# Two of four weight-block sums of a seven-product square built by an accumulating DMA from GpSimd instead of VectorE

## The chip, the cores and the metric

The kernel runs on 1 core of one Trainium2 chip. The metric is the device time of one execution in microseconds. The kernel before took 1205.96 us (median of 3 runs, 1202.22 to 1206.86).

## What is computed

One decoder layer on 256 tokens of width 2048: a mixer (pooling heads and RWKV-7 heads), then a squared-ReLU MLP, then a gate with per-layer embeddings, and a final norm. All weights and activations are float32. The change lies in the MLP:

```python
h2 = rms_norm(x, mlp_norm[i])
x = x + jnp.square(jax.nn.relu(h2 @ w_ffn_up[i])) @ w_ffn_down[i]
```

with `w_ffn_up` 2048 x 8192 and `w_ffn_down` 8192 x 2048.

## The kernel before, in words

**Precision.** TensorE multiplies fp32r operands. To keep float32 accuracy each operand is split into a high part (ScalarE copies it to fp32r, `wh`) and a low part (VectorE subtracts the copy from the source, `wl`). A product is three matmuls: high x high, high x low, low x high (L1100 to L1102). So every weight that is loaded costs one or two ScalarE copies (128x512 each) and one VectorE subtraction (128x1024) before TensorE can use it.

**Stages.** The mixer comes first. Then the MLP runs in two halves of the 8192 hidden columns (`ffn_half`, L1172). Each half computes FFN-up for eight groups of hidden columns (`gemm_wide`), squares them, and then makes two sweeps of FFN-down (`down_sweep`, L1078), one for each 1024 of the 2048 output columns: sweeps 1 and 2 for the first half, 3 and 4 for the second. The last sweep also keeps weights for the gate (`keep`, L1039) and transposes the residual for the next stage (L1007, `between`).

**A sweep** goes over 16 squares (`kp`, L1122). A square is 256 tokens by 256 hidden rows by 1024 output columns, seen as 2 x 2 blocks. The weights of a square are two raw tiles, rx and ry, of 128 x 1024 float32 (512 KB each); rx holds W11 and W12, ry holds W21 and W22, each 128 x 512. They are loaded on SyncE's queue into a pool of three buffers (`load_raw`, L140). Ten squares (twelve in the last sweep) take the ordinary eight block products, 24 matmuls. The squares in `SEVEN` = 1, 3, 6, 8, 11, 13 (1, 3, 6, 11 in the last sweep; 22 in all) use a Strassen-Winograd form with seven products, 21 matmuls. For it the activations are summed while FFN-up runs (`activation_sums`, L1063), and the weights in the sweep by VectorE, in the tile `t_` (one buffer of 128 x 2048, slot a1):

```python
t1 = W12 - W11          # L1140
t3 = W22 - W12          # L1141
t2 = t3 + W11           # L1142
t4 = W21 - t2           # L1143
```

Then t1 and t3 are split together (`halves_of` "c", L1111 and L1112), and t2 and t4 (`halves_of` "d", into own tiles). The split tiles `wh` and `wl` of the pool have three buffers each.

**Order of the work.** Every engine works through a queue of its own in order. The Tile framework makes that order when the kernel is built, by program order and priorities (`tc.high_priority`), and adds the semaphore waits that the data and the buffers need. SyncE's queue holds the loads; a load waits for the buffer it writes. GpSimd's queue is used only at the start, for constants.

**After the last seven-product square of a sweep** (L1155 to L1167) the products that only the seven-product form fills are added to the residual `xr` with the scale `s2` (`add`, L1120); s2 is the inverse mean square of the norm, computed once in the first half of FFN-up (`inv_ms`, L1028). The other four banks are added at the end of the sweep.

Of the kernel before, what the change touches and what calls it, by code (L numbers as in the profile page):

```python
# [9 lines left out]
F32 = mybir.dt.float32  # L10
F32R = mybir.dt.float32r
AF = mybir.ActivationFunctionType
ALU = mybir.AluOpType
# [27 lines left out]
def trunk(  # L41
# [19 lines left out]
    nc = tc.nc  # L61

    const = ctx.enter_context(tc.tile_pool(name="const", bufs=1))
# [6 lines left out]
    def mm_bank(name):  # L70
        return psm.tile([128, 512], F32, tag="mm", name=name)
# [68 lines left out]
    def load_raw(src, n, name):  # L140
        raw = wp.tile([128, 1024], F32, tag="raw", name=f"raw_{name}")
        nc.sync.dma_start(raw[:, 0:n], src)
        return raw
# [11 lines left out]
    def split_sb(h_ap, l_ap, src_ap):  # L155
        nc.scalar.activation(h_ap, src_ap, AF.Copy)  # L156
        nc.vector.tensor_tensor(l_ap, src_ap, h_ap.bitcast(F32), op=ALU.subtract)  # L157
# [93 lines left out]
    def a8(slot, name, dt=F32):  # L251
        return act.tile([128, 2048], dt, tag=f"a{slot}", name=name)
# [713 lines left out]
    fp = ctx.enter_context(tc.tile_pool(name="fp", bufs=1))  # L966
# [57 lines left out]


    s2 = const.tile([128, 2], F32, name="s2sq")

    def inv_ms():  # L1028
        ss2 = rms_stat(xr, "n2")
        nc.vector.tensor_scalar(s2, ss2, 1.0 / D, NORM_EPS, op0=ALU.mult, op1=ALU.add)  # L1030
        nc.vector.reciprocal(s2, s2)

    h3_box = []

# [22 lines left out]

    SEVEN = (1, 3, 6, 8, 11, 13)  # L1060
    s_slots = (0, 2, 5)

    def activation_sums(box, kp, r):  # L1063

        i = SEVEN.index(kp)
        if i % 2 == 0:
            box[kp] = box[SEVEN[min(i + 1, len(SEVEN) - 1)]] = a8(s_slots[i // 2], f"S{kp}", F32R)
        st = box[kp][:, i % 2 * 1024 : i % 2 * 1024 + 1024]
        t_ = fp.tile([128, 1024], F32, tag="junk", bufs=1, name=f"s{kp}")
        s1, s2_, s3, s4 = (t_[:, j * 128 : (j + 1) * 128] for j in range(4))  # L1070
        a11, a21, a12, a22 = (r[:, j * 128 : (j + 1) * 128] for j in range(4))
        nc.vector.tensor_tensor(s1, a21, a22, op=ALU.add)
        nc.vector.tensor_tensor(s3, a11, a21, op=ALU.subtract)
        nc.vector.tensor_tensor(s2_, s1, a11, op=ALU.subtract)
        nc.vector.tensor_tensor(s4, a12, s2_, op=ALU.subtract)
        split_sb(st[:, 0:512], st[:, 512:1024], t_[:, 0:512])

    def down_sweep(hf, pair, ys, sboxes, hooks=(), between=None, seven=SEVEN):  # L1078

        nm = f"d{hf}{pair}"  # L1080
        hooks = dict(hooks)
        b2, b4, b3, bx = (mm_bank(f"{nm}_b{i}") for i in range(4))
        w16, w57 = (wide_bank(f"{nm}_w{i}") for i in range(2))
        b1, b6, b5, b7 = w16[:, 0], w16[:, 1], w57[:, 0], w57[:, 1]
        todo = {"2": 0, "3": 0, "4": 0, "x": 0, "1": 0, "5": 0, "6": 0, "7": 0}
        banks = {"2": b2, "3": b3, "4": b4, "x": bx, "1": b1, "5": b5, "6": b6, "7": b7}
        for kp in range(16):
            if kp in seven:
                for n in "1234567":
                    todo[n] += 1  # L1090
            else:
                for n in "234x":
                    todo[n] += 2
        left = dict(todo)

        def prod(n, a_, w_):
            first, last = left[n] == todo[n], left[n] == 1
            left[n] -= 1
            (ah, al), (wh, wl) = a_, w_
            nc.tensor.matmul(banks[n], ah, wh, start=first, stop=False)  # L1100
            nc.tensor.matmul(banks[n], ah, wl, start=False, stop=False)  # L1101
            nc.tensor.matmul(banks[n], al, wh, start=False, stop=last)  # L1102

        def halves_of(src, name, own=False):

            pool, kw = (fp, dict(bufs=2)) if own else (wp, {})
            wh = pool.tile([128, 1024], F32R, tag="graw" if own else "wh", name=f"wh_{name}", **kw)
            wl = pool.tile([128, 1024], F32R, tag="graw" if own else "wl", name=f"wl_{name}", **kw)
            with tc.high_priority(20000):
                for c in range(2):  # L1110
                    nc.scalar.activation(wh[:, c * 512 : c * 512 + 512], src[:, c * 512 : c * 512 + 512], AF.Copy)  # L1111
                nc.vector.tensor_tensor(wl, src, wh.bitcast(F32), op=ALU.subtract)  # L1112
            return [(wh[:, c * 512 : c * 512 + 512], wl[:, c * 512 : c * 512 + 512]) for c in range(2)]

        def xs(tt, c):
            o = pair * 1024 + c * 512
            return xr[tt][:, o : o + 512]

        def add(tt, c, src):
            nc.vector.scalar_tensor_tensor(xs(tt, c), src, s2[:, tt : tt + 1], xs(tt, c), op0=ALU.mult, op1=ALU.add)  # L1120

        for q, kp in enumerate((0, 2, 1, 4, 3, *range(5, 16)) if pair else range(16)):  # L1122
            if q in hooks:
                hooks[q]()
            y, j = ys[kp // 2], kp % 2 * 512
            a11, a21, a12, a22 = ((y[:, j + i * 128 : j + i * 128 + 128], y[:, 1024 + j + i * 128 : 1152 + j + i * 128]) for i in range(4))
            rx, ry = (load_raw(w_down[pair, hf * 32 + 2 * kp + i], 1024, f"{nm}_{kp}_{i}") for i in range(2))
            if kp in seven:
                i = SEVEN.index(kp)
                st = sboxes[kp][:, i % 2 * 1024 : i % 2 * 1024 + 1024]  # L1130
                s1, s2_, s3, s4 = ((st[:, c * 128 : c * 128 + 128], st[:, 512 + c * 128 : 640 + c * 128]) for c in range(4))
                t_ = a8(1, f"t{nm}_{kp}")
                t1, t3, t2, t4 = (t_[:, c * 512 : c * 512 + 512] for c in range(4))
                wa = fp.tile([128, 1024], F32R, tag="wa", name=f"wa{nm}_{kp}")
                w11 = wa[:, 0:512], wa[:, 512:1024]
                with tc.high_priority(20000):
                    split_sb(*w11, rx[:, 0:512])
                w21, w22 = halves_of(ry, f"{nm}_{kp}b")
                with tc.high_priority(20000):
                    nc.vector.tensor_tensor(t1, rx[:, 512:1024], rx[:, 0:512], op=ALU.subtract)  # L1140
                    nc.vector.tensor_tensor(t3, ry[:, 512:1024], rx[:, 512:1024], op=ALU.subtract)  # L1141
                    nc.vector.tensor_tensor(t2, t3, rx[:, 0:512], op=ALU.add)  # L1142
                    nc.vector.tensor_tensor(t4, ry[:, 0:512], t2, op=ALU.subtract)  # L1143
                w1, w3 = halves_of(t_[:, 0:1024], f"{nm}_{kp}c")
                w2, w4 = halves_of(t_[:, 1024:2048], f"{nm}_{kp}d", True)
                for n, a_, w_ in (("1", a11, w11), ("2", a12, w21), ("3", s4, w22), ("5", s1, w1), ("7", s3, w3), ("6", s2_, w2), ("4", a22, w4)):
                    prod(n, a_, w_)
            else:
                w11, w12 = halves_of(rx, f"{nm}_{kp}a")
                for n, a_, w_ in (("2", a11, w11), ("4", a21, w11), ("3", a11, w12), ("x", a21, w12)):  # L1150
                    prod(n, a_, w_)
                w21, w22 = halves_of(ry, f"{nm}_{kp}b")
                for n, a_, w_ in (("2", a12, w21), ("4", a22, w21), ("3", a12, w22), ("x", a22, w22)):
                    prod(n, a_, w_)
            if kp == seven[-1]:  # L1155
                add(0, 0, b1)
                u = fp.tile([128, 512], F32, tag="r", bufs=2, name=f"u{nm}")
                nc.scalar.activation(u, b1, AF.Copy)
                nc.vector.tensor_tensor(u, b6, u, op=ALU.add)
                add(0, 1, u)  # L1160
                add(0, 1, b5)
                nc.vector.tensor_tensor(u, b7, u, op=ALU.add)
                add(1, 0, u)
                add(1, 1, u)
                add(1, 1, b5)
                if between is not None:
                    between()  # L1167
        for n, tt, c in (("2", 0, 0), ("4", 1, 0), ("3", 0, 1), ("x", 1, 1)):
            with tc.high_priority(30000):
                add(tt, c, banks[n])  # L1170

    def ffn_half(hf):  # L1172
        sboxes = {}
        ys = []
        for i in range(8):
# [3 lines left out]
            def square(bi, bank):  # L1179
# [5 lines left out]
                split_sb(y[:, bi * 512 : bi * 512 + 512], y[:, 1024 + bi * 512 : 1024 + bi * 512 + 512], r)  # L1185
                if 2 * i + bi in SEVEN:
                    activation_sums(sboxes, 2 * i + bi, r)
# [167 lines left out]
```

## Time and profile before

| | us |
|---|---|
| median of 3 runs | 1205.96 (1202.22 to 1206.86) |
| the profiled execution's own time | 1200.63 |
| its span, first to last instruction | 1198.9 |
| TensorE (PE) busy in the span | 1179.6 (98%) |
| VectorE (DVE) busy | 868.1 (72%) |
| ScalarE (ACT) busy | 687.7 (57%) |
| GpSimd (POOL) busy | 15.4 (1%) |

In the rows of the profile PE is TensorE's matmuls and PEld its weight loads, DVE VectorE, ACT ScalarE, POOL GpSimd, SP SyncE; a "q" behind a name means the engine's queue, and L1142 is line 1142 of the kernel. A group's row has the line, the engine, the operation, out<-in by the program's tile names, the shapes and the count. A tile's row has the duration in ns as minimum/median/maximum and the first and last start. A row of the timeline has start us, duration us, engine, line, operation and, in brackets, the idle time before it and what ended that. A row of waits has who waited for what: us in total, times, longest. A row of DMA issues has the tile, the queue, the count, KB each and the median us from issue to landing. The sweeps lie at 570 to 738 us (1 and 2) and 916 to 1089 us (3 and 4).

### The profile page before, as it was taken

How to read it: one execution, taken by the hardware profiler on the slowest of the kernel's cores; microseconds unless marked ns; L12 is line 12 of the kernel's file. 1: busy time of each engine (PE TensorE's matmuls, PEld its weight loads, DVE VectorE, ACT ScalarE, POOL GpSimd, SP SyncE). 2: the span in 40 equal slices, each digit the busy share in tenths (PEclk: the TensorE clock that was granted, in tenths of full speed). 3: DMA queues.
4: the chain of work that ended last, by engine and by line, in shares of the span. 5: the costliest groups of instructions: out<-in, count | busy, mean ns of one | idle time of the engine just before them, and what ended most of it. 6: DMA issues, size and time to landing. Idle time of an engine off the chain costs nothing.

```text
span 1198.9 us, 18442 instructions
## 1 busy us (share of the span) xinstructions
PE 1179.6 (98%) x7076; PEld 1013.6 (85%) x7076; DVE 868.1 (72%) x1150; ACT 687.7 (57%) x1260; POOL 15.4 (1%) x65
## 2 busy tenths in 40 slices
PE   8999999999999999999999999999999999999996
PEld 6999988988888888888888788888888888778886
DVE  8687987854556667666888878666667888887552
ACT  6857565665545556555555555555555655668544
POOL 4000000000000000000000000000000000000000
PEclk9999999999999999999999999999999999999999
DMA  7463542354355565666665666665565655776631
GB/s 250 151 202 110 173 155 95 121 186 142 116 177 169 185 185 191 192 193 189 194 203 197 197 197 203 195 187 189 192 193 178 211 198 191 290 234 219 194 121 71
DMA packets 60328, 216.88 MB, mean 181 GB/s; under 512 B 6736, under 2 KB 7120, under 8 KB 59856
## 3 DMA queue, kind: packets, MB, share of 16 engines
q1 hardware_dynamic: 59952, 215.19, 55.1%
q8 instruction: 55, 0.90, 0.3%
q10 hardware_dynamic: 288, 0.52, 0.1%
q14 instruction: 33, 0.27, 0.1%
HBM read 213.59 MB, written 2.10 MB: 180 GB/s over the span
## 4 chain that ended last, share of the span: by engine, by line
PE 81%; DMA 6%; DVE 6%; ACT 4%; issue 2%; SPq 0%; ACTq 0%; DVEq 0%
PE u_w L986 20%; PE u_w L990 10%; DMA raw_d<-in_w_ffn_down_dram 5%; PE d_b L1101 4%; PE d_b L1100 4%; PE d_b L1102 4%; PE gt_b L173 2%; PE gt_b L175 2%; PE gt_b L174 2%; PE zv_b L164 1%; PE zp_b L173 1%; PE wag_b L333 1%; PE zv_b L165 1%; PE zv_b L166 1%; PE zp_b L175 1%
## 5 line engine op out<-in xcount | busy, mean ns | idle before, releaser
L986 PE MATMUL u_w<-h,wh_u 128*128 128x512 f32 x1024 | 355.4, 393 | 0.0
L990 PE MATMUL u_w<-h,wl_u 128*128 128x256 f32 x1024 | 285.5, 279 | 0.0
L151 ACT ACTIVATE wh_u<-raw_u 128x512 fp32r<-128x512 f32 x256 | 147.6, 624 | 162.9 <-PE u_w L986 82.0
L152 DVE TENSOR_TENSOR wl_u<-raw_u,wh_u 128x1024 fp32r<-128x1024 f32 x128 | 156.6, 1224 | 112.1 <-ACT wh_u L151 112.1
L986 PEld LDWEIGHTS u_w<-h,wh_u 128*128 128x128 f32 x1024 | 191.8, 187 | 43.2
L990 PEld LDWEIGHTS u_w<-h,wl_u 128*128 128x128 f32 x1024 | 193.1, 189 | 0.1
L152 DVE TENSOR_TENSOR wl_gt<-raw_gt,wh_gt 128x1024 fp32r<-128x1024 f32 x24 | 29.4, 1225 | 23.9 <-ACT wh_gt L151 23.9
L151 ACT ACTIVATE wh_gt<-raw_gt 128x512 fp32r<-128x512 f32 x48 | 27.8, 631 | 23.0 <-PE gt_b L175 20.4
L1140 DVE TENSOR_TENSOR td<-raw_d 128x512 f32<-128x512 f32 x22 | 15.2, 692 | 33.9 <-DMA raw_d<-in_w_ffn_down_dram 33.9
L164 PE MATMUL zv_b<-hTh,wh_zv 128*128 128x256 f32 x128 | 37.7, 294 | 0.0
L173 PE MATMUL gt_b<-wh_gt,h 128*128 128x512 f32 x96 | 37.5, 390 | 0.0
L164 PE MATMUL zr_b<-hTh,wh_zr 128*128 128x256 f32 x128 | 37.5, 293 | 0.0
L175 PE MATMUL gt_b<-wh_gt,h 128*128 128x512 f32 x96 | 37.4, 389 | 0.0
L174 PE MATMUL gt_b<-wl_gt,h 128*128 128x512 f32 x96 | 37.4, 389 | 0.0
L166 PE MATMUL zr_b<-hTh,wl_zr 128*128 128x256 f32 x128 | 37.2, 290 | 0.1
L164 PE MATMUL zk_b<-hTh,wh_zk 128*128 128x256 f32 x128 | 37.0, 289 | 0.0
L165 PE MATMUL zr_b<-hTl,wh_zr 128*128 128x256 f32 x128 | 36.9, 288 | 0.0
L165 PE MATMUL zk_b<-hTl,wh_zk 128*128 128x256 f32 x128 | 36.3, 284 | 0.5 <-DVE hTl L157 0.5
L166 PE MATMUL zk_b<-hTh,wl_zk 128*128 128x256 f32 x128 | 36.3, 284 | 0.2 <-DVE wl_zk L152 0.2
L166 PE MATMUL zv_b<-hTh,wl_zv 128*128 128x256 f32 x128 | 36.2, 283 | 0.0
L165 PE MATMUL zv_b<-hTl,wh_zv 128*128 128x256 f32 x128 | 36.2, 283 | 0.0
L156 ACT ACTIVATE wad<-raw_d 128x512 fp32r<-128x512 f32 x22 | 13.9, 632 | 36.6 <-DMA raw_d<-in_w_ffn_down_dram 34.5
(804 smaller groups left out, 3081.4 us busy)
## 6 DMA issues: line engine op xcount, KB each, us to landing
raw_u<-in_w_ffn_up_dram SPq DMA_DIRECT2D x128, 512.0 KB, 3.5
raw_d<-in_w_ffn_down_dram SPq DMA_DIRECT2D x128, 512.0 KB, 4.2
raw_gt<-in_w_ple_gate_dram SPq DMA_DIRECT2D x24, 512.0 KB, 3.5
raw_zk<-in_w_in_dram SPq DMA_DIRECT2D x16, 512.0 KB, 3.3
raw_zr<-in_w_in_dram SPq DMA_DIRECT2D x16, 512.0 KB, 3.3
raw_zv<-in_w_in_dram SPq DMA_DIRECT2D x16, 512.0 KB, 3.3
raw_zp<-in_w_in_dram SPq DMA_DIRECT2D x16, 512.0 KB, 3.2
raw_o<-in_w_out_dram SPq DMA_DIRECT2D x16, 512.0 KB, 3.5
```

The source lines that it names most:

```text
L151: nc.scalar.activation(wh[:, a * 512 : (a + 1) * 512], raw[:, a * 512 : (a + 1) * 512], AF.Copy)
L152: nc.vector.tensor_tensor(wl, raw, wh.bitcast(F32), op=ALU.subtract)
L164: nc.tensor.matmul(o, w_h, ah, start=first and ct % 2 == 0, stop=False, skip_group_check=True)
L165: nc.tensor.matmul(o, w_h, al, start=False, stop=False, skip_group_check=True)
L166: nc.tensor.matmul(o, w_l, ah, start=False, stop=last, skip_group_check=True)
L173: nc.tensor.matmul(o, a_h, wh[:, 0:n], start=first, stop=False)
L174: nc.tensor.matmul(o, a_h, wl[:, 0:n], start=False, stop=False)
L175: nc.tensor.matmul(o, a_l, wh[:, 0:n], start=False, stop=last)
L986: nc.tensor.matmul(bank[:, ct, :].rearrange("p (s t) -> p s t", s=2), wh[:, c], hl, start=k == 0, stop=False, skip_group_check=True,)
L990: nc.tensor.matmul(bank[:, ct, 0:T], wl[:, c], hl[:, 0, :], start=False, stop=k == 15, skip_group_check=True)
L1100: nc.tensor.matmul(banks[n], ah, wh, start=first, stop=False)
L1101: nc.tensor.matmul(banks[n], ah, wl, start=False, stop=False)
```

## The change

The signs of the seven-product form are turned so that the first two weight sums are plain additions: t1 = W11 + W12, t3 = W12 + W22, t2 = t3 + W11, t4 = W21 + t2. The activation sums turn two signs (L1072, L1075), and two of the additions to the residual take a negative scale `ns2` (`take`).

t1 and t3 are now made by DMA, issued from GpSimd: a plain load of the whole row of tile ke (W11 and W12) into one half of `t_`, and then an accumulating load that adds W12 and W22 onto it. `t_` is allocated once a sweep and its two halves of 128 x 1024 take turns; `weight_sums` for the first seven-product square is issued at the start of the sweep, and for each following one while the square before it is set up. VectorE still makes t2 and t4, in a tile `t24` (tag "junk", one buffer, shared with the activation sums and the squares of the norm). In a seven-product square rx now loads W11 only (256 KB).

```diff
+        nc.vector.tensor_scalar_mul(ns2, s2, -1.0)
...
-        nc.vector.tensor_tensor(s1, a21, a22, op=ALU.add)
+        nc.vector.tensor_tensor(s1, a21, a22, op=ALU.subtract)
...
-        nc.vector.tensor_tensor(s4, a12, s2_, op=ALU.subtract)
+        nc.vector.tensor_tensor(s4, a12, s2_, op=ALU.add)
...
+        t_ = a8(1, f"t{nm}")
+        t13s = {}
+
+        def weight_sums(kp):
+
+            ke, o = hf * 32 + 2 * kp, len(t13s) % 2 * 1024
+            t13 = t13s[kp] = t_[:, o : o + 1024]
+            nc.gpsimd.dma_start(t13, w_down[pair, ke])
+            nc.gpsimd.dma_start(
+                t13.rearrange("p (a n) -> p a n", a=2), w_down[pair, ke : ke + 2, :, 512:1024].rearrange("a p n -> p a n"),
+                accum_op=ALU.add,
+            )
+
+        weight_sums(seven[0])
+        def take(tt, c, src):
+            nc.vector.scalar_tensor_tensor(xs(tt, c), src, ns2[:, tt : tt + 1], xs(tt, c), op0=ALU.mult, op1=ALU.add)
...
-            rx, ry = (load_raw(w_down[pair, hf * 32 + 2 * kp + i], 1024, f"{nm}_{kp}_{i}") for i in range(2))
+            ke = hf * 32 + 2 * kp
+            rx = load_raw(w_down[pair, ke, :, 0 : 512 if kp in seven else 1024], 512 if kp in seven else 1024, f"{nm}_{kp}_0")
+            ry = load_raw(w_down[pair, ke + 1], 1024, f"{nm}_{kp}_1")
...
-                t_ = a8(1, f"t{nm}_{kp}")
-                t1, t3, t2, t4 = (t_[:, c * 512 : c * 512 + 512] for c in range(4))
+                t13, t3 = t13s[kp], t13s[kp][:, 512:1024]
+                t24 = fp.tile([128, 1024], F32, tag="junk", bufs=1, name=f"t{nm}_{kp}")
+                t2, t4 = t24[:, 0:512], t24[:, 512:1024]
+                if len(t13s) < len(seven):
+                    weight_sums(seven[len(t13s)])
...
-                    nc.vector.tensor_tensor(t1, rx[:, 512:1024], rx[:, 0:512], op=ALU.subtract)
-                    nc.vector.tensor_tensor(t3, ry[:, 512:1024], rx[:, 512:1024], op=ALU.subtract)
                     nc.vector.tensor_tensor(t2, t3, rx[:, 0:512], op=ALU.add)
-                    nc.vector.tensor_tensor(t4, ry[:, 0:512], t2, op=ALU.subtract)
-                w1, w3 = halves_of(t_[:, 0:1024], f"{nm}_{kp}c")
-                w2, w4 = halves_of(t_[:, 1024:2048], f"{nm}_{kp}d", True)
+                    nc.vector.tensor_tensor(t4, ry[:, 0:512], t2, op=ALU.add)
+                w1, w3 = halves_of(t13, f"{nm}_{kp}c")
+                w2, w4 = halves_of(t24, f"{nm}_{kp}d", True)
...
-                add(0, 1, u)
+                take(0, 1, u)
                 add(0, 1, b5)
                 nc.vector.tensor_tensor(u, b7, u, op=ALU.add)
                 add(1, 0, u)
-                add(1, 1, u)
+                take(1, 1, u)
```

More of the change, by code (lines that the diff above doesn't have):

```diff
@@ L1026, in trunk @@
     s2 = const.tile([128, 2], F32, name="s2sq")
+    ns2 = const.tile([128, 2], F32, name="ns2sq")
     def inv_ms():
```

## The prediction

> **What bounds the kernel now.** I read the table of stretches first, cut at the four FFN-down sweeps. Its columns are the stretch in us, its length, then busy us (and instructions) of PE, PEld, DVE, ACT and POOL, the granted TensorE clock, the DMA share and GB/s.
>
> ```profile
> 569.90:654.00 84.10, 84.10 (x373) 69.47 (x372) 70.86 (x81) 48.62 (x86) 0.00 (x0) 1.00 0.62 200
> 654.00:738.00 84.00, 82.87 (x362) 67.22 (x361) 70.27 (x78) 46.54 (x82) 0.00 (x0) 1.00 0.63 195
> 738.00:904.00 166.00, 166.00 (x959) 145.03 (x958) 111.57 (x137) 86.42 (x154) 0.00 (x0) 1.00 0.60 192
> 904.00:990.00 86.00, 86.00 (x397) 71.80 (x396) 68.97 (x77) 50.63 (x89) 0.00 (x0) 1.00 0.61 198
> 990.00:1085.00 95.00, 92.27 (x411) 75.10 (x410) 80.66 (x93) 58.15 (x107) 0.00 (x0) 1.00 0.72 241
> ```
>
> Sweeps 1 and 2 are the first two rows; sweeps 3 and 4 lie in the last two (the fourth row begins with the end of FFN-up). TensorE is busy through all of rows 1, 3 and 4, at a clock of 1.00. It lacks 84.00 − 82.87 = 1.13 us in row 2 and 95.00 − 92.27 = 2.73 us in row 5: **3.9 us is all that the sweeps can give back**. The waits of TensorE say to whom (us, times, longest):
>
> ```profile
> PE h3t L1007 <- DVE x L1120: 1.3, 1, 1.3
> PE h3t L1007 <- DVE ud L1159: 0.8, 1, 0.8
> PE d_w L1101 <- DVE wl_d_6d L1112: 0.6, 1, 0.6
> ...
> PE d_b L1101 <- DVE wl_d_12b L1112: 0.4, 1, 0.4
> PE d_b L1101 <- DVE wl_d_6b L1112: 0.3, 1, 0.3
> PE d_w L1101 <- DVE wl_d_6c L1112: 0.2, 1, 0.2
> ...
> PE d_b L1101 <- DVE wl_d_7b L1112: 0.2, 1, 0.2
> ```
>
> The last five rows, 1.7 us, are weight parts that VectorE delivered late in or behind a seven-product square. The first two, 2.1 us, are the transposes in sweep 4 that wait for the residual. Together 3.8 us, the 3.9 again.
>
> Then I asked why VectorE is late, from its timeline in sweep 2 and its and SyncE's waits:
>
> ```profile
> 664.62 1.22 DVE L1112 TENSOR_TENSOR wl_d_1c<-td,wh_d_1c 128x1024 fp32r<-128x1024 f32 x1
> ...
> 669.13 0.69 DVE L1140 TENSOR_TENSOR td<-raw_d 128x512 f32<-128x512 f32 x1 [1.02 <-DMA raw_d<-in_w_ffn_down_dram]
> ...
> 679.79 0.69 DVE L1140 TENSOR_TENSOR td<-raw_d 128x512 f32<-128x512 f32 x1 [1.38 <-DMA raw_d<-in_w_ffn_down_dram]
> ...
> 683.79 0.69 DVE L1142 TENSOR_TENSOR td<-td,raw_d 128x512 f32<-128x512 f32 x1
> ```
> ```profile
> DVE td L1140 <- DMA raw_d<-in_w_ffn_down_dram: 33.9, 20, 3.6
> ```
> ```profile
> SPq L142 <- DVE td L1142: 39.8, 22, 4.6
> ```
>
> VectorE idles 33.9 us for weights although it is the late engine. It is a loop: SyncE can load the next raw tile only when one of three buffers is free; the buffer of rx is held until L1142, which needs ry as well (39.8 us of SyncE's waiting); so the next rx lands late and L1140 waits. From kp=3 to kp=6 (669.13 to 679.79) one turn, a square with seven products and one with eight, takes VectorE 10.66 us. TensorE needs 45 matmuls for it; the pace is in these two rows, 12 matmuls apart:
>
> ```profile
> 572.67 0.39 PE L1100 MATMUL d_b<-wh_d_0b,y 128*128 128x512 f32 x1
> ...
> 575.39 0.39 PE L1100 MATMUL d_w<-wad,y 128*128 128x512 f32 x1
> ```
>
> (575.39 − 572.67)/12 = 0.227 us, so 10.2 us a turn. The loop is 0.45 us too slow there and makes it good where two eight-product squares follow each other. That is the whole deficit.
>
> **The change part by part.**
>
> ```profile
> L1140 DVE TENSOR_TENSOR td<-raw_d x22: 682/693/694, 567.7 to 1052.8; 128x512 f32<-128x512 f32 x22
> L1141 DVE TENSOR_TENSOR td<-raw_d,raw_d x22: 682/686/694, 570.5 to 1055.1; 128x512 f32<-128x512 f32 x22
> ```
> ```profile
> raw_d<-in_w_ffn_down_dram SPq DMA_DIRECT2D x60, 512.0 KB, 4.1
> ```
>
> *Removed*: L1140 and L1141, 0.693 + 0.686 = 1.38 us of VectorE in each of 22 squares, 30 us in all. Almost all of it lies under TensorE, so it counts only through the 3.8 us. The loop gets better by more than the 1.38 us: the second sum now comes from DMA, so L1142 no longer needs ry, and rx is freed right behind its own landing. With 1.38 us less in a turn whose excess is 0.45, the loop is faster than TensorE. The split of the first two sums needs no raw tile at all and can fill the idle time. I count the five weight waits as gone: **−1.7 us**. Late next would be the transposes of sweep 4. Their first wait is for VectorE's first additions, and VectorE comes to them straight from square 11, without idle time in between:
>
> ```profile
> 1059.43 1.22 DVE L1112 TENSOR_TENSOR wl_d_11d<-td,wh_d_11d 128x1024 fp32r<-128x1024 f32 x1
> 1060.56 1.22 DVE L1112 TENSOR_TENSOR wl_d_12a<-raw_d,wh_d_12a 128x1024 fp32r<-128x1024 f32 x1
> 1061.82 1.23 DVE L1112 TENSOR_TENSOR wl_d_12b<-raw_d,wh_d_12b 128x1024 fp32r<-128x1024 f32 x1
> 1062.96 0.74 DVE L1120 SCALAR_TENSOR_TENSOR x<-d_w,s2sq,x 128x512 f32<-128x512 f32 x1
> ```
>
> 1.38 us less ahead of 1062.96 covers the 0.8 us wait and a little of the 1.3; the rest hangs on the chain of additions itself, which stays. **−1.0 us.**
>
> *Added on GpSimd's queue*: 22 plain loads of 512 KB and 22 accumulating ones of 512 KB; rx shrinks by 256 KB. Net 768 KB a square, 17.3 MB. The pair is ordered (the second waits for the first), and behind that wait only the next pair is queued; POOL has no instruction in any of the rows above. The tile has two halves, so the sums of a square may start when the split of the square two before is over: sweep 2 splits kp=1 until 664.62 + 1.22 = 665.84 and would need kp=6's sum at 683.79, **18 us** later. The trace has no DMA issued by GpSimd and no accumulating one. Nearest row below: a plain 512 KB load, 4.1 us. Nearest above, a 512 KB load among four others:
>
> ```profile
> DMA packets 873, 3.71 MB, mean 337 GB/s; under 512 B 99, under 2 KB 99, under 8 KB 744
> ...
> q1 hardware_dynamic: 872, 3.69, 88.0%
> ...
> raw_d<-in_w_ffn_down_dram SPq DMA_DIRECT2D x3, 512.0 KB, 5.2
> ...
> graw<-in_w_ple_gate_dram SPq DMA_DIRECT2D x1, 512.0 KB, 6.4
> ```
>
> (from 1025 to 1036 us). A pair is thus 8.2 to 12.8 us, and up to 6.4 + 12.8 = 19 us if accumulating doubles the disturbed row. Squares come every 84.1/6 = 14 us, so up to 14 us a pair the queue keeps up and the sums are in time. I take 10 us, near the undisturbed row, with the accumulating load somewhat dearer than the plain one. Cost on the path: 0; upwards, rival B.
>
> The Trainium skill ("DMA: Bandwidth & Descriptors", Measured and Anatomy of one DMA) gives GpSimd's path 2.0 us plus bytes over 436 GB/s; the estimate by that page is 3.2 us a load and 6.4 us a pair, which leaves the sum as it is; it has no price for an accumulating load, and no run here shows either yet.
>
> *What it does to the raw loads.* In sweep 1, six squares bring 6 × 0.79 = 4.7 MB more in 84 us: 200 GB/s become 256, and 293 if the accumulating loads' read of their target counts like their bytes. The rows above show 337 GB/s at a share of 88% with raw landings of 5.2 us instead of 4.1. Bounds of the raw landing: 4.1 to 6.4 us. I take one collision in each turn at +1.1 us, which eats most of what the loop gained but not all. Residue in late parts: **+0.2 us**, between 0 and the rival's price.
>
> *Nothing counted*: the two remaining sums with changed signs and the `take` rows cost what they did (same shapes); `ns2` is one small instruction in FFN-up, where VectorE is busy 111.57 of 166.00 us; t24 moves to "junk", whose other users are in FFN-up. Without that cover each would cost under 1 us.
>
> Sum: −1.7 − 1.0 + 0.2 = **−2.5 us**. The profiled execution took 1200.63 us (span 1198.9, 1.7 around it) and would take 1198.1. It lies under the runs shown (1202.22 to 1206.86); carried to their median, 1205.96 − 2.5 = **1203.5 us**.
>
> **The rivals.**
>
> *A, raw loads slowed (slower).* GpSimd's transfers share the DMA engines with SyncE's. If most raw loads of a turn take 6.4 instead of 4.1 us: four raws through three buffers put 4/3 of a landing into a turn, 2.3 × 4/3 = 3.1 us, against a gain of 1.4 to 2. With the 0.45 excess a turn loses about 1.5 us, 22 turns 33 us, of which the double eight-product stretches (3 of 6 in a sweep) win back half: +16 us, **1222**. It decides from about +1.5 us on the landing of every raw load. For: graw's 6.4 us, and row 5 has 241 GB/s already. Against: the mean of 256 to 293 is under the 337 seen.
>
> *B, sums late (slower).* If a pair takes over 14 us, GpSimd's queue falls behind by the difference at each square; the lead of 18 us is soon gone, and then t2 waits in VectorE's in-order queue, with all later splits behind it and TensorE behind them. At 17 us a pair it is up to 3 us × 22 = 66 us, **1272**. The same holds if the pair is not issued ahead of its square. The Trainium skill ("SBUF — State Buffer", Who interferes with whom) says that VectorE's two-port modes starve GpSimd's descriptor writing, and that tensor_tensor has no such mode. By the first half B would follow, with VectorE busy 70.86 of 84.10 us; by the second not. The rows speak for the second: 0.69 us for 512 and 1.22 for 1024 columns, the same 1.04 ns a column in each.
>
> *C, nothing moves.* The late parts stay, because landings eat what the loop gained: **1206**.
>
> *D, all waits go*, both transposes' too: −3.8, **1202**; over 0.5% (6 us) faster is beyond the 3.9 us of idle time.
>
> **How the numbers follow.** 0.5%, about 6 us, is what a measurement of this kernel can tell from no change. Forecast 0.47, A 0.25, B 0.06, C 0.15, D 0.07. The time is the forecast's, 1203.5, with a range of its own from 1200 to 1207. The whole range leaves out B, the upper third of A and a little below D: 1198.5 to 1224. Same: forecast, C and nearly all of D, 0.65; faster 0.05, for a median of other runs and an unforeseen order of instructions; slower A and nearly all of B, 0.30.
>
> **What would show it.** Right: the PE rows in the waits with wl_d_… gone, VectorE's busy time 30 us down, L1142's share in SyncE's waits down, raw_d under 5 us to landing. Wrong: t2 waiting for a DMA from GpSimd (B); raw_d over 5.6 us and wh_d waiting for DMA in every square (A); PE rows that stay at equal landings (C).

## The result, and the profile after

The changed kernel takes 1224.06 us (median of 4 runs, 1222.93 to 1225.8); the kernel before, run beside it, 1205.54 us (4 runs, 1202.22 to 1206.86). The ratio is 1.0166, with a 95% interval of 1.0146 to 1.0186: **slower by 18.5 us**, where 2.5 us less was forecast. It is rival A's direction, and about 2 us off its price.

The page of the changed kernel: the span, the busy time of the engines, the DMA queues (packets, MB, share of 16 engines), the chain of work that ended last, and the DMA issues.

```profile
span 1221.2 us, 18549 instructions
...
PE 1190.1 (97%) x7076; PEld 1016.4 (83%) x7076; DVE 841.0 (69%) x1107; ACT 683.4 (56%) x1260; POOL 54.9 (4%) x109
...
q1 hardware_dynamic: 59952, 209.42, 51.6%
q0 software_dynamic: 9152, 23.07, 8.2%
...
PE 75%; DMA 9%; DVE 8%; ACT 5%; issue 3%; SPq 0%; DVEq 0%; ACTq 0%
...
raw_d<-in_w_ffn_down_dram SPq DMA_DIRECT2D x106, 512.0 KB, 4.7
td<-in_w_ffn_down_dram POOLq DMA_DIRECT2D x44, 512.0 KB, 6.0
raw_d<-in_w_ffn_down_dram SPq DMA_DIRECT2D x22, 256.0 KB, 3.9
```

The same row of the chain in the kernel before:

```profile
PE 81%; DMA 6%; DVE 6%; ACT 4%; issue 2%; SPq 0%; ACTq 0%; DVEq 0%
```

VectorE did lose its work: 868.1 to 841.0 us of busy time. Yet more of the chain that sets the end runs through DMA (6% to 9%) and less through TensorE. The stretches say where. Sweeps 1 and 2, then 3 and 4, of the kernel before (stretch, length, then busy us of PE, PEld, DVE, ACT and POOL, granted clock, DMA share, GB/s):

```profile
570.00:738.00 168.00, 166.87 (x732) 136.59 (x731) 141.02 (x158) 95.16 (x167) 0.00 (x0) 1.00 0.63 198
916.00:1089.00 173.00, 170.27 (x756) 139.64 (x755) 145.93 (x165) 104.16 (x186) 0.00 (x0) 1.00 0.67 225
```

and of the changed kernel:

```profile
575.00:751.00 176.00, 169.65 (x732) 135.89 (x731) 125.00 (x133) 92.14 (x166) 20.18 (x24) 1.00 0.80 240
929.00:1110.00 181.00, 172.98 (x754) 140.19 (x753) 131.23 (x141) 100.79 (x183) 14.27 (x16) 0.99 0.78 247
```

The sweeps grow from 341 to 357 us, **16 us, and this is the effect**. VectorE has 31 us less to do in them (286.95 to 256.23), and the DMA engines go from shares of 0.63 and 0.67 to 0.80 and 0.78. Of the 16 us, TensorE's idle time takes 10.5: it grows from 3.9 us (341 − 337.14) to 14.4 (357 − 342.63). The other 5.5 us stand in the rows as longer busy time for as many matmuls (1488 and 1485 in the rows); what makes them longer is not shown. Between the two profiled executions lie 22.3 us (1200.63 and 1222.93); the other 6 lie outside the sweeps, 3.3 of them in the first half of FFN-up, where the pace of the matmuls differs (last section).

The waits of TensorE in the changed kernel, in the sweeps:

```profile
PE d_w L1104 <- DVE wl_d_6d L1115: 3.2, 1, 3.2
PE h3t L1007 <- DVE x L1123: 2.0, 2, 1.8
PE d_b L1104 <- DVE wl_d_5a L1115: 1.9, 2, 1.0
PE d_w L1104 <- DVE wl_d_3c L1115: 1.7, 3, 0.6
PE d_w L1104 <- DVE wl_d_8c L1115: 1.7, 3, 0.6
PE d_w L1104 <- DVE wl_d_6c L1115: 1.2, 2, 0.6
PE d_b L1104 <- DVE wl_d_6b L1115: 1.2, 1, 1.2
```

In part they are the late parts of before (6b, 6c, 6d and the transposes), only later and more often; 5a, 3c and 8c are new. Who made VectorE and ScalarE late:

```profile
DVE td L1166 <- DMA raw_d<-in_w_ffn_down_dram: 34.5, 18, 3.8
DVE td L1165 <- DMA raw_d<-in_w_ffn_down_dram: 29.6, 18, 2.9
```
```profile
ACT wad L156 <- DMA raw_d<-in_w_ffn_down_dram: 37.7, 19, 3.8
```

VectorE waited 33.9 us at L1140 for raw tiles; now L1165 and L1166, the two sums left to it, wait 34.5 + 29.6 = 64 us, both for raw_d. Much of this is hidden under TensorE: without the transfers (e1, below) the same two sums wait 25.1 + 18.3 = 43 us and cost nothing. No row has VectorE waiting for td from DMA: the sums of GpSimd's queue are in time, so rival B does not happen. The margin is small in places: in three of the 22 squares the sums landed under 1 us before L1165 started.

**One collision.** VectorE's timeline in sweep 2 (the sums of squares 3 and 6), the issues on GpSimd's queue, the DMA issues of 689 to 699 us, and stretches of 5 us:

```profile
674.33 0.69 DVE L1165 TENSOR_TENSOR td<-td,raw_d 128x512 f32<-128x512 f32 x1 [0.18 <-DMA raw_d<-in_w_ffn_down_dram]
...
687.72 0.69 DVE L1165 TENSOR_TENSOR td<-td,raw_d 128x512 f32<-128x512 f32 x1 [2.07 <-DMA raw_d<-in_w_ffn_down_dram]
...
694.77 0.69 DVE L1166 TENSOR_TENSOR td<-raw_d,td 128x512 f32<-128x512 f32 x1 [3.48 <-DMA raw_d<-in_w_ffn_down_dram]
```
```profile
686.01 0.59 POOL L1132 DMA_DIRECT2D td<-in_w_ffn_down_dram  x1 [6.19 <-DVE wl_d_3c L1115]
690.13 1.17 POOL L1133 DMA_DIRECT2D td<-in_w_ffn_down_dram  x1 [3.53 <-DMA td<-in_w_ffn_down_dram]
```
```profile
raw_d<-in_w_ffn_down_dram SPq DMA_DIRECT2D x3, 512.0 KB, 5.9
td<-in_w_ffn_down_dram POOLq DMA_DIRECT2D x1, 512.0 KB, 9.9
```
```profile
680.00:685.00 5.00, 4.90 (x21) 3.49 (x19) 3.54 (x4) 3.76 (x7) 0.00 (x0) 1.00 1.04 261
685.00:690.00 5.00, 3.50 (x15) 2.54 (x15) 2.93 (x4) 2.19 (x4) 0.59 (x1) 1.00 0.69 205
690.00:695.00 5.00, 5.00 (x24) 4.12 (x23) 1.51 (x3) 0.24 (x1) 1.17 (x1) 1.00 0.82 222
695.00:700.00 5.00, 3.19 (x13) 2.04 (x12) 3.96 (x4) 3.52 (x7) 0.25 (x1) 1.00 0.94 251
```

At 689.57, 690.17 and 691.31 us SyncE issues three raw loads, because its three buffers come free almost together; GpSimd issues the accumulating load into the middle, at 690.13. It lands after 9.9 us, the raw loads after 5.9 (median) instead of 4.1. VectorE, which needs ry at L1166, idles 3.48 us; TensorE is busy 3.19 of the next 5 us. Ahead of that, at L1165, VectorE idled 2.07 us for rx, although the next raw tile of square 5 had landed at 683.17 and ScalarE had copied it by 684.7: in the changed order VectorE's part of its split (5a) stands behind L1165, where before it stood ahead of L1140. From kp=3 to kp=6, L1165 starts 687.72 − 674.33 = 13.4 us apart, where one turn of the kernel before took 10.66 and TensorE needs 10.2. The shares near 1 (a little over it, so read it as full) come with 251 to 261 GB/s in this collision, far under the 337 GB/s at 88% of the prediction's row.

### The profile page after: what moved, and what is told of

The parts are those of the page before. It is cut to its first block, busy times and chain, and to the rows that moved or that the text cites. A ratio compares the mean times of both kernels' runs of the same rounds, so it can differ in the third digit from the quotient of the medians.

```text
span 1221.2 us, 18549 instructions
## 1 busy us (share of the span) xinstructions
PE 1190.1 (97%) x7076; PEld 1016.4 (83%) x7076; DVE 841.0 (69%) x1107; ACT 683.4 (56%) x1260; POOL 54.9 (4%) x109
## 3 DMA queue, kind: packets, MB, share of 16 engines
q0 software_dynamic: 9152, 23.07, 8.2%
## 4 chain that ended last, share of the span: by engine, by line
PE 75%; DMA 9%; DVE 8%; ACT 5%; issue 3%; SPq 0%; DVEq 0%; ACTq 0%
PE u_w L986 19%; PE u_w L990 10%; DMA raw_d<-in_w_ffn_down_dram 8%; PE d_b L1104 3%; PE d_b L1103 3%; PE d_b L1105 3%; PE gt_b L173 2%; PE gt_b L174 2%; PE gt_b L175 2%; PE zv_b L164 1%; PE zp_b L173 1%; PE zv_b L165 1%; PE zv_b L166 1%; PE zp_b L175 1%; PE zp_b L174 1%
## 5 line engine op out<-in xcount | busy, mean ns | idle before, releaser
L1132 POOL DMA_DIRECT2D td<-in_w_ffn_down_dram x22 | 13.0, 592 | 752.1 <-DVE wl_d_1c L1115 430.4
L1166 DVE TENSOR_TENSOR td<-raw_d,td 128x512 f32<-128x512 f32 x22 | 15.2, 692 | 34.5 <-DMA raw_d<-in_w_ffn_down_dram 34.5
```

## The experiments

The expectations use names. **Theory 1**: the loss comes with GpSimd's transfers, which slow the raw loads; 1a, it is their latency, which three buffers cannot hide; 1b, the DMA engines are full. **Theory 2**: it is the order in VectorE's queue, which splits b, d, c in a seven-product square where it split b, c, d before, so that the ready sums idle behind ry. **Theory 3**: it is the accumulating, more than the bytes; 3a, the adding itself; 3b, its packets of 2 KB. All in one table; "sweeps" is the length of the four sweeps, and "DMA time" the sum of share times length, both from the two stretches that cover them (the kernel before: 0.63 × 168 + 0.67 × 173 = 222 us). Each ratio is to runs of the kernel before on the same chip in the same session, whose medians were 1203.23 to 1205.54 us.

| kernel | median us | ratio to before (95%) | sweeps us | DMA time us |
|---|---|---|---|---|
| before | 1205.54 | | 341 | 222 |
| after | 1224.06 | 1.0166 (1.0146 to 1.0186) | 357 | 282 |
| e1_sums_free | 1205.92 | 1.0013 (0.9997 to 1.0029) | 338 | 208 |
| e2_plain_second | 1210.91 | 1.0062 (1.0044 to 1.0079) | 344 | 256 |
| e7_acc_alone | 1235.59 | 1.0237 (1.0197 to 1.0277) | 365 | 263 |
| e8_swap | 1231.34 | 1.0226 (1.0197 to 1.0255) | 365 | 285 |
| e4_c_first | 1224.87 | 1.0166 (1.0146 to 1.0187) | 358 | 283 |
| e5_traffic | 1256.47 | 1.0437 (1.0420 to 1.0455) | 392 | 304 |
| e11_traffic_plain | 1235.18 | 1.0260 (1.0226 to 1.0294) | 369 | 280 |
| e10_traffic_more_raw | 1247.86 | 1.0361 (1.0325 to 1.0397) | 382 | 300 |
| e6_more_raw | 1269.26 | 1.0524 (1.0487 to 1.0561) | 399 | 285 |
| e9_signs | 1207.80 | 1.0018 (1.0000 to 1.0036) | 340 | 225 |
| v1_before_more_raw | 1203.09 | 0.9977 (0.9960 to 0.9995) | 336 | 213 |

### e1_sums_free: the changed kernel almost without GpSimd's transfers

```diff
-            nc.gpsimd.dma_start(t13, w_down[pair, ke])
-            nc.gpsimd.dma_start(..., accum_op=ALU.add)
+            if len(t13s) <= 2:
+                nc.gpsimd.dma_start(t13, w_down[pair, ke])
```

> The changed kernel, but GpSimd loads each half of the sum tile only once a sweep (plain, 8 loads in all) and never accumulates; all squares of a sweep use these tiles, so the products 5, 7, 6 and 4 are computed from wrong sums. VectorE's and TensorE's work and their order stay. Theory 1 (transfers collide with the raw loads): the loss goes with the transfers, 1203 us, at most 1206. Theory 2 (the order in which VectorE splits the sums, second pair ahead of the first, makes TensorE wait): the loss stays for the larger part, 1214 us or more, and the waits for the first pair's low parts (5.9 us) stay.

Measured 1205.92 us. Its sweeps (one stretch for each pair) and the waits of TensorE that are left in them:

```profile
574.00:741.00 167.00, 166.22 (x733) 136.86 (x732) 126.58 (x134) 93.93 (x166) 2.10 (x4) 1.00 0.58 194
922.00:1093.00 171.00, 169.63 (x758) 140.26 (x757) 133.17 (x144) 101.98 (x184) 1.06 (x2) 1.00 0.65 219
```
```profile
PE h3t L1007 <- DVE x L1123: 1.4, 1, 1.4
PE d_w L1104 <- DVE wl_d_6c L1115: 0.6, 1, 0.6
...
PE d_b L1104 <- DVE wl_d_6b L1115: 0.2, 1, 0.2
```

The sweeps are 338 us, 3 under the kernel before: a gain of the size that the prediction counted (2.7) is there, with the order b, d, c and all else of the change in place. The 19 us up to the changed kernel's 357 come with the transfers. (The kernel as a whole does not gain. In the traced execution FFN-up ran at the slower of two paces and took 6.6 us more than in the kernel before, last section; that this holds for all ten runs is not shown.)

### e2_plain_second: the second load plain

```diff
-                accum_op=ALU.add,
```

> The changed kernel, but the second load of a pair is plain, not accumulating, so that it overwrites the first and the products 5, 7, 6 and 4 use wrong sums. The bytes read from memory are the same. Theory 1 with the bytes as the cause: at most 3 us under the changed kernel, 1221 to 1224. Theory 3 (it is the accumulating that holds the DMA engines; its landing took 6 to 10 us, the plain one's 4): half of the loss or more goes, 1206 to 1215, and raw_d lands in 4.3 us instead of 4.7.

Measured 1210.91 us; its queue and issues:

```profile
q0 software_dynamic: 6336, 23.07, 5.6%
...
raw_d<-in_w_ffn_down_dram SPq DMA_DIRECT2D x106, 512.0 KB, 4.3
td<-in_w_ffn_down_dram POOLq DMA_DIRECT2D x44, 512.0 KB, 4.9
```

The same 23.07 MB cost 344 − 338 = 6 us of the sweeps as plain loads, and 13 more when half of them accumulate. The queue's share prices the two kinds: here 5.6% of a span of 1208.9 us is 67.7 us, 1.54 us of the 16 engines for each of 44 loads. In the changed kernel 8.2% of 1221.2 is 100.1 us; less 22 × 1.54 = 33.9, 66.2 us remain for 22 accumulating loads, **3.0 us each, twice a plain load's** for the same bytes.

### e7_acc_alone: only the accumulating loads

```diff
-            nc.gpsimd.dma_start(t13, w_down[pair, ke])
+            if len(t13s) <= 2:
+                nc.gpsimd.dma_start(t13, w_down[pair, ke])
             nc.gpsimd.dma_start(..., accum_op=ALU.add)
```

> The changed kernel without the plain loads (one for each half of the sum tile at the start of a sweep is left); the 22 accumulating loads stay and add onto whatever stands in the tile, so that the products 5, 7, 6 and 4 use wrong sums. In the profile of the changed kernel GpSimd's 44 loads took 8.2% of 16 engines' span, and in the run with two plain loads 5.6%: an accumulating load holds the engines about 3.0 us, a plain one 1.5. If only that time counts, one accumulating load costs like two plain ones: 1208 to 1213. If accumulating disturbs the raw loads beyond its time: 1215 or more.

Measured 1235.59 us, dearer than the changed kernel although 14 loads are gone (q0 moves 15.73 MB). VectorE's and ScalarE's waits for raw tiles grow further (L1167 is here the sum that L1166 was, t4):

```profile
DVE td L1167 <- DMA raw_d<-in_w_ffn_down_dram: 43.1, 16, 5.1
```
```profile
ACT wad L156 <- DMA raw_d<-in_w_ffn_down_dram: 56.6, 20, 7.5
```

So it is not the DMA time alone (263 us here): an accumulating load that comes without the plain one ahead of it is issued some 4 us earlier. That it then falls among the square's own raw loads, and costs more by that, was only argued; the median landing of the whole raw rows is 4.7 us in both kernels.

### e8_swap: the accumulating load in long rows

```diff
-            nc.gpsimd.dma_start(t13, w_down[pair, ke])
             nc.gpsimd.dma_start(
                 t13.rearrange("p (a n) -> p a n", a=2), w_down[pair, ke : ke + 2, :, 512:1024].rearrange("a p n -> p a n"),
-                accum_op=ALU.add,
             )
+            nc.gpsimd.dma_start(t13, w_down[pair, ke], accum_op=ALU.add)
```

> The changed kernel with the two GpSimd loads of a sum exchanged: the plain one brings the two blocks in rows of 2 KB ([W12|W22]), the accumulating one adds the contiguous row of 4 KB ([W11|W12]); the sums and the bytes are the same. Queue q0 shows 272 packets for an accumulating load of rows of 2 KB and 144 for either plain load. If the cost of accumulating lies in its packets of 2 KB (theory 3b), the accumulating load drops to about 144 packets, its landing from about 8 to 5-6 us, and the time to 1212-1217 us. If it lies in the adding itself (theory 3a), the landings stay, and the time stays at 1222-1227 us.

Measured 1231.34 us.

```profile
q0 software_dynamic: 6336, 23.07, 8.4%
...
raw_d<-in_w_ffn_down_dram SPq DMA_DIRECT2D x106, 512.0 KB, 5.0
td<-in_w_ffn_down_dram POOLq DMA_DIRECT2D x44, 512.0 KB, 7.7
```

The packets fall from 9152 to 6336, 144 a load for either kind, and nothing gets cheaper: 8.4% of 1230.0 us is 103.3 us, (103.3 − 33.9)/22 = 3.2 us an accumulating load. Theory 3b falls; the adding itself (3a) takes the time. That the exchange is 7 us dearer still, beyond the 1222 to 1227 expected, is not explained.

### e4_c_first: c split ahead of b

```diff
+                w1, w3 = halves_of(t13, f"{nm}_{kp}c")
                 w21, w22 = halves_of(ry, f"{nm}_{kp}b")
...
-                w1, w3 = halves_of(t13, f"{nm}_{kp}c")
...
-                for n, a_, w_ in (("1", a11, w11), ("2", a12, w21), ("3", s4, w22), ("5", s1, w1), ("7", s3, w3), ("6", s2_, w2), ("4", a22, w4)):
+                for n, a_, w_ in (("1", a11, w11), ("5", s1, w1), ("7", s3, w3), ("6", s2_, w2), ("4", a22, w4), ("2", a12, w21), ("3", s4, w22)):
```

> The changed kernel with the split of the first pair of sums put ahead of ry's and the seven products in the order 1, 5, 7, 6, 4, 2, 3, the order in which VectorE then delivers the parts (first pair, second pair, ry). Same transfers. Theory 1: the loss stays, 1220 to 1226. Theory 2: 1212 or less, and no wait of TensorE for the first pair's low part.

Measured 1224.87 us, the changed kernel's time. Theory 2 falls: the idle time can be filled with the split of the sums (VectorE's waits at the two sums fall from 64 to 29.9 + 13.9 = 44 us), but what comes behind it is as late as before. Here 5a also stands ahead of the next t2 again, so that order is not the cause either.

### e5_traffic, e11_traffic_plain, e10_traffic_more_raw: the transfers on the kernel before

In e5 the kernel before also issues the changed kernel's 22 pairs of loads, into a tile that nothing reads; each pair but a sweep's first is held back by a small GpSimd copy of the square's split W11. In e11 the second load is plain. In e10 the loads are e5's, and rx of a seven-product square has a buffer of its own (the edit of v1, below).

```diff
+        jk = fp.tile([128, 1024], F32, tag="junk", bufs=1, name=f"jk{nm}")
+
+        def more_traffic(kp, after=None):
+            if after is not None:
+                nc.gpsimd.tensor_copy(jk[:, 0:1], after[:, 1023:1024].bitcast(F32))
+            ke = hf * 32 + 2 * kp
+            nc.gpsimd.dma_start(jk, w_down[pair, ke])
+            nc.gpsimd.dma_start(jk..., accum_op=ALU.add)
```

> The kernel before, with the 22 pairs of GpSimd loads (plain, then accumulating) added, into a tile that nobody reads; each pair waits until the square before has split W11. VectorE makes all sums as before. Theory 1: the whole loss comes without the change, 1217 to 1226, with raw_d landing in 4.7 us or more. Theory 2: 1205 to 1209.

> e5_traffic with the second load of each pair plain instead of accumulating: the kernel before with 44 plain GpSimd loads of 512 KB into a tile that nobody reads. e5_traffic took 1256.5 us, 51 above before. If it is the accumulating that disturbs the raw loads (theory 3, two thirds of the loss in the changed kernel), this lies at 1215-1228 us, raw loads at 4.2-4.4 us; if the bytes alone do it (theory 1), it stays at 1245 us or more.

> The kernel before with the 22 pairs of GpSimd loads into a tile that nobody reads (as in e5_traffic, 1256.5 us) and with the first row of a square of seven products in a buffer of its own (as in v1, 1203.1 us). Nothing waits for the GpSimd loads here. If the loss comes from the latency of the raw loads that three buffers cannot hide (theory 1a), a fourth buffer takes off most of it: below 1230 us. If the DMA engines are full during the sweeps (theory 1b), the buffer changes little: above 1245 us.

e5 took 1256.47 us, e11 1235.18, e10 1247.86. The transfers alone, with VectorE's work as before and nobody reading what they bring, cost more than in the changed kernel, whose rx is half as large. But one stall in sweep 4 belongs to the edit itself: the extra loads write the slot "junk", a single buffer that the squares of the next norm (L260) need as well. The first of these waits on ScalarE, with the splits of square 7 behind it. First ScalarE's wait in e5, then TensorE's in e10, then e10's two sweep pairs:

```profile
ACT junk_n L260 <- issue: 15.5, 1, 15.5
```
```profile
PE d_b L1100 <- ACT wh_d_7a L1111: 12.9, 1, 12.9
```
```profile
574.00:761.00 187.00, 171.73 (x730) 137.97 (x729) 142.73 (x161) 94.98 (x168) 24.65 (x30) 0.98 0.79 241
942.00:1137.00 195.00, 175.10 (x756) 140.12 (x755) 144.64 (x163) 102.11 (x185) 20.64 (x25) 0.96 0.78 245
```

"issue" means that the profile names nobody, but the times do: the last extra load of the sweep lands at 1088.47 us in e5, 1080.54 in e10 and 1067.54 in e11, and the squares start 0.14 to 0.15 us later each time. TensorE stands still for it 16.7 us in e5, 12.9 in e10 and 6.8 in e11. Less the stall of its trace, e5's median comes to 1239.8 us, e10's to 1235.0 and e11's to 1228.4. So e10's result above 1245 is the stall's doing; 1235 lies between its two expected values, and the sweeps have to decide.

Without the stall the sweeps are longer than those of the same kernel without the loads by 392 − 16.7 − 341 = 34 us in e5, 382 − 12.9 − 336 = 33 in e10, and 369 − 6.8 − 341 = 21 in e11. The fourth buffer takes off nothing. That does not settle theory 1a against 1b: in e10 VectorE waits 50.7 us for raw tiles at the sum t3 (L1162), which needs ry, where the same sum waits 25.4 us in v1, and ry still goes through the three buffers. Latency that one buffer more cannot hide and engines that are full for stretches (the mean share is 0.79 and 0.78) both fit; more buffers than one were not tried. Accumulating instead of plain loads costs 34 − 21 = 13 us here as well, as between e2 and the changed kernel.

e11 missed both of its expectations, and without the stall it lies at the upper edge of the first. The plain bytes cost 21 us here and 6 in e2. The DMA time differs in the same direction, 280 us against 256, but it cannot be the whole reason: e7, with 263 us, has sweeps of 365.

### e6_more_raw: W11 in buffers of its own

```diff
-            rx = load_raw(w_down[pair, ke, :, 0 : 512 if kp in seven else 1024], 512 if kp in seven else 1024, f"{nm}_{kp}_0")
+            if kp in seven:
+                rx = fp.tile([128, 512], F32, tag="rx7", bufs=2, name=f"raw_{nm}_{kp}_0")
+                nc.sync.dma_start(rx, w_down[pair, ke, :, 0:512])
+            else:
+                rx = load_raw(w_down[pair, ke], 1024, f"{nm}_{kp}_0")
```

> The changed kernel with two buffers more for weights in the sweeps: W11 of the seven-product squares is loaded into tiles of its own (two of 256 KB) and the other raw tiles keep the three buffers. Same transfers by GpSimd. Theory 1a (the collisions lengthen landings, and the three buffers cannot hide that): the loss falls to 8 us or less, 1204 to 1213. Theory 1b (the DMA engines as such are full): it stays, 1219 or more.

The two buffers are those that `ph` and `pl` use at the end. Measured 1269.26 us. That lies in the range of theory 1b, but the loss has another cause:

```profile
DVE td L1169 <- DMA td<-in_w_ffn_down_dram: 60.9, 13, 7.1
...
DVE td L1170 <- DMA raw_d<-in_w_ffn_down_dram: 38.5, 18, 4.1
```

With W11 there early, the addition t2 (L1169) moves ahead in VectorE's queue and waits there for the accumulating load, 60.9 us, with the later splits behind it. This is rival B's wait in another kernel. That the time comes near B's price (1272) is chance: the price was worked out from pairs that take 17 us, and here t2 comes early instead. So e6 says nothing on theories 1a and 1b.

### e9_signs and v1_before_more_raw: the kernel before with one edit

e9 has only the turned signs (subtract and add exchanged, `ns2` and `take`), all four sums on VectorE.

> The kernel before with the signs of the changed form alone: all four sums still made by VectorE, the negative scale added, no DMA by GpSimd. Every theory: no difference, 1202 to 1208.

Measured 1207.80 us, sweeps 340 us: in the sweeps the signs cost nothing.

v1 gives rx of the seven-product squares a buffer of its own, which `ph` and `pl` use at the end:

```diff
+            if kp in seven:
+                rx = fp.tile([128, 1024], F32, tag="rx7", name=f"raw_{nm}_{kp}_0")
+                nc.sync.dma_start(rx, w_down[pair, ke])
+            else:
+                rx = load_raw(w_down[pair, ke], 1024, f"{nm}_{kp}_0")
```

> The kernel before with one buffer more: rx of the seven-product squares is loaded into a tile of its own, ry and all others keep the three. If the waits of the kernel before come from the loop of raw buffers, the sweeps lose 2 to 3 us: ratio 0.997 to 0.999. If they come from VectorE's work, nothing moves: ratio 1.000.

Measured 1203.09 us, ratio 0.9977 (0.9960 to 0.9995); of TensorE's waits in the sweeps one row is left:

```profile
PE h3t L1007 <- DVE x L1120: 0.2, 1, 0.2
```

The sweeps are 5 us shorter, a little more than the 3.9 us that the prediction took for all that they can give. So the loop of rx's buffer, as the prediction read it, was the cause of the waits before, and this edit cures it without a byte more. It is the fastest version here, by 0.2% of the time, with an interval that only just leaves out 1.

### b2_before: a second trace of the kernel before

> The kernel before, unchanged, for a second trace of it. If the pace of FFN-up (a pair of matmuls in 345-349 ns or in 351-355 ns at a granted clock of 1.00) is drawn at each execution, its two halves may show 181.6 or 180.9 us here where the first trace shows 178.3 and 177.5; if it belongs to the program, both come out at 178 us again.

One execution, 1200.02 us; both halves of FFN-up came out at 178 us again. Its use is in the last section.

## Why the prediction was wrong

- **What bounds the kernel: right.** TensorE's 3.8 us of waits, VectorE behind a loop of raw buffers: v1 removes the loop, and all but 0.2 us of the waits goes. Only "all that the sweeps can give back" was low: 3.9 us, against 5 in v1.
- **The gain: about right, and lost again.** −1.7 − 1.0 = −2.7 us was counted; e1, the change without its transfers, has sweeps 3 us shorter. Its waits fall by less than was counted: 0.6 + 0.2 us of weight parts and 1.4 us of transposes are left of 1.7 and 2.1.
- **The pair on GpSimd's queue: a little low, without effect.** 10 us were taken. The timeline has 690.13 − 686.01 = 4.1 us from the first issue to the second, and the second landed after 9.9: 14 us in that case; by the medians of 22 each, a plain load lands after 3.9 us and an accumulating one after 8.0, so 12 for a pair. It lies in the bounds (8.2 to 19), and no sum was waited for.
- **The raw loads: the step that failed.** "I take one collision in each turn at +1.1 us" and "+0.2 us" for the residue. The +1.1 was the right size: read one by one in the trace, the whole rows among the raw loads land after 4.2 us (median of 38) with no accumulating load in flight and after 5.4 (68 loads) with one. The count was wrong: of all 128 raw loads 82 meet one, not one in each of 22 turns, for an accumulating load is in flight 8 of the 14 us between squares; and some take far longer, up to 9.7 us. This term cost 357 − 338 = 19 us of the sweeps, not 0.2.
- **Why it was sized so: by bytes.** 256 GB/s, or 293 with the reads of the target, looked safe under 337. In engine time an accumulating load takes twice a plain one's for its bytes (3.0 against 1.5 us). The mean share came to 0.80 and 0.78, with stretches at 0.94 to 1.04 that carry only 251 to 261 GB/s in the collision above. Whether the engines' time or the few buffers make the loss out of it stays open (e10).
- **Rival A: the mechanism, its price by other numbers.** +16 us was worked out from all landings at 6.4 us; +16 was measured, with a median of 4.7 for the whole rows. So "it decides from about +1.5 us on the landing of every raw load" is wrong, and the sign "raw_d under 5 us to landing" of a right forecast was met by a slower kernel. By the traces the mean landing of the whole rows went from 4.14 to 4.99 us; by the prediction's own 4/3 that is 1.1 us a turn, under the 1.4 to 2 that the loop had gained. That the few late loads set the loop, and not the median, fits the collision above, but no run parts the two. The nearness of the price is luck.
- **"The split of the first two sums needs no raw tile at all and can fill the idle time".** In the changed kernel it does not: VectorE's queue has b, d, c. Made to (e4), it gains nothing.
- **Rival B: excluded for the right reason here** (the lead suffices, in three squares by under 1 us), and its wait is shown in e6, when t2 comes early in VectorE's queue. Its "1.04 ns a column in each" is the step between the two rows, (1.22 − 0.69)/512 us; each row by itself gives 1.35 and 1.19 ns.
- **"junk", "whose other users are in FFN-up": wrong, without effect here.** The squares of the next norm use it in sweep 4; they waited 0.2 us for it in the changed kernel, and 15.5 us in e5.

The Trainium skill ("DMA: Bandwidth & Descriptors", Issuing engines are not separate DMA queues) says that transfers started from different engines run on the same 16 DMA engines and interleave. The runs agree: nobody reads what e5's loads bring, and beside the one stall they lengthen the sweeps by 34 us. The estimate of 3.2 us a load by that page's figures is under the 4.2 us that e1's plain GpSimd loads took:

```profile
td<-in_w_ffn_down_dram POOLq DMA_DIRECT2D x4, 512.0 KB, 4.2
```

## What to carry to other kernels

Work that moves from a compute engine to DMA has a price in engine time of the DMA engines in that stage, not only in bytes against a bandwidth: take the queue's share, divide by its loads, add it to the stage's DMA share, and expect waits well before the mean reaches 1 (here at 0.8). The sum is no forecast by itself: e7 has less DMA time than the changed kernel and loses more, so when the transfers are issued counts as well. An engine with idle time and a late input is helped little by less work (3 us of the sweeps in e1); find what its input waits for, here a buffer that was held too long, which a tile more cures (5 us in v1). A tile that is added to a test must not share a buffer with the work, or the test measures that. A median landing time does not show the late loads.

## What the runs showed of the hardware that was not expected

- **An accumulating load costs twice.** 3.0 to 3.2 us of the 16 engines for 512 KB against 1.54 for a plain one, at 272 or at 144 packets (e8); GpSimd's issue takes 1.18 instead of 0.59 us in the changed kernel, and 0.88 instead of 0.75 in e8, where the accumulating load has the long rows.
- **A long stall also costs clock.** In e5's stall TensorE stands still for 10 us at a granted clock of 0.50, and the next 10 us have 0.78:

```profile
1080.00:1090.00 10.00, 0.00 (x0) 0.00 (x0) 0.00 (x0) 1.38 (x3) 1.22 (x1) 0.50 0.44 102
1090.00:1100.00 10.00, 9.66 (x34) 7.82 (x35) 5.95 (x5) 6.26 (x12) 0.00 (x0) 0.78 0.65 238
```

- **FFN-up has two paces at full clock.** In the same 160 us of FFN-up, with TensorE busy throughout, the kernel before makes 925 matmuls and the changed one 908; first the kernel before, then the changed one:

```profile
400.00:560.00 160.00, 160.00 (x925) 141.15 (x924) 106.56 (x133) 88.01 (x158) 0.00 (x0) 1.00 0.60 189
```
```profile
400.00:560.00 160.00, 160.00 (x908) 139.03 (x907) 105.38 (x133) 86.89 (x156) 0.00 (x0) 1.00 0.58 186
```

A half of FFN-up takes about 178 or about 181 us in the traces, and either half of one execution may be the slow one. The kernel before was at the fast pace in both of its traces, e9 (signs alone) at the slow one, with 908 matmuls in that stretch. Of the twelve traces of the changed kernel and the edited ones, ten have the slow pace in the first half and nine in the second. Whether this belongs to a program or to an execution stays open: the two traces of the kernel before agree, but the kernel before's own runs spread from 1199.55 to 1209.54 us. It blurs every comparison here by some 3 us for each half of FFN-up, which is why the sweeps were compared.
